# A hybrid decoder block on one core: x and mem loaded as columns, row scales put on the results, GpSimd taken out of two places

## The chip, the cores and the metric

The kernel runs on one core of a Trainium2 chip. A core has a matrix engine (TensorE, PE in the profile, with its weight loads as PEld), a vector engine (VectorE, DVE), an activation engine (ScalarE, ACT), a general engine (GpSimd, POOL) and SyncE (SP), which here issues every transfer between DRAM and on-chip memory. On-chip memory is SBUF (128 partitions) and PSUM (eight banks, where TensorE puts its sums). The metric is the device time of one execution in microseconds (us); the median of a kernel's runs is compared.

## The reference

All data is float32: x is 256 tokens of 1024 features, mem is 256 tokens of 1024.

```python
def rms_norm(x, g):
    y = xf * lax.rsqrt(jnp.mean(xf * xf, axis=-1, keepdims=True) + EPS)
    return (y * g)
h = x
hn = rms_norm(h, norm_mix)
(gq, gk, gv, gr, glr, nq, kc, vc, ks_, vs_, kw, vw, ng) = _split_cols(hn @ w_in)
o_gla = gla_mixer(gq, gk, gv, gr, glr, ...)      # 4 heads, chunked linear attention with decay
o_nsa = nsa_mixer(nq, kc, vc, ks_, vs_, kw, vw, ng, ...)  # 8 heads: compressed, selected, window
h = h + concat([o_gla, o_nsa]) @ w_out
h = h + cross_attn(rms_norm(h, norm_xattn), rms_norm(mem, norm_mem), ...)
h = h + peer_ffn(rms_norm(h, norm_ffn), ...)     # 8 heads pick 16 of 16384 experts per token
return rms_norm(h, norm_final)
```

The norm divides a row (a token) by its root mean square and multiplies a column (a feature) by g. A projection of the normed rows is therefore r(token) times (x * g) @ w: the row scale r can be applied after the projection as well as before it.

## The kernel before

**Numbers.** Every large product is done in three TensorE passes: each float32 factor is split in a high part (a rounded copy, made on ScalarE, line 137) and a low part (source minus high part, line 138, on VectorE or, where `eng` is P, on GpSimd); lines 152 to 154 multiply high by high, and the two mixed pairs. `weights` loads a 512 KB block of weights into one of four `raw` buffers and splits it into `whi` and `wlo`. `proj_t` multiplies one such block (8 pieces of 128 features) with the activations `xh`, `xl`, which lie as columns (feature on the partition, 256 tokens beside each other); its 24 products fill one of the two `pj` banks. `proj_n` does the same with tokens on the partition of the result.

**Stages, in the order of the program.**

1. x is loaded as rows (four DMAs), squared on ScalarE with the sums kept (line 170), `rstd_of` makes the row scale r by logarithm, exponential and one Newton step (lines 159 to 165); `norm_t` multiplies x by r and g (line 193, VectorE), turns it by TensorE transposes (line 197) and splits it into `xh`, `xl`.
2. `w_tok` (4 blocks of 296 KB, low parts on GpSimd) gives `tok`; `w_t` blocks 0 to 3 give qT and kT of the linear attention (scaled copies from PSUM on ScalarE). The gate goes from `tok` by transposes (line 297) and two products (line 304) to the decay.
3. Two rounds (d = 0 and 1) of linear attention: seven levels each, three or four VectorE operations per level (lines 366, 368, 373) between TensorE products (line 372). TensorE fills the time with `proj_t` blocks that are due later.
4. mem is loaded, normed and turned in the same way (lines 384 to 394) into `mh`, `ml`; compressed keys (lines 405 to 459), then queries nq and keys sk, copied out of PSUM by ScalarE.
5. Sparse attention, gates and output norm, cross-attention's keys and values, the output product, the norm between, cross-attention; `residual` adds each product to h and does the next norm. There `norm_t` of both halves is on the path: TensorE has nothing else that it may start.
6. PEER: eight `peer_wq` blocks (low parts on GpSimd), the search for the best keys on VectorE (`best`), then 128 `down_t` blocks, 256 weight maps and 128 `up` blocks. `gates_exp` needs another ScalarE table than the Gelu between whose uses it stands.
7. The last norm (lines 917 to 941): VectorE adds h, ScalarE squares, GpSimd multiplies by g (line 932), VectorE or ScalarE scales, four DMAs store.

**What sets the order.** The order on each engine is fixed when the program is built: the framework's scheduler lists the instructions by their dependences and its own estimate of times. `tc.issue_after(i)` adds that an instruction on i's engine stands behind i. SP issues all loads in one fixed order; a load into a `raw` buffer stands and waits until the buffer's last reader is done, and all that is behind it waits as well. `t8` tiles share two 8 KB buffers in turn, so mem's load waits for the second round of linear attention to let go of one.

## Time and profile before

| | us |
|---|---|
| median of 3 runs | 1105.44 (1105.41 to 1106.59) |
| profiled execution | 1104.22 |
| its span, first to last instruction | 1102.3 |
| TensorE busy | 1070.7 (97%) |
| VectorE busy | 775.8 (70%) |
| ScalarE busy | 583.8 (53%) |
| GpSimd busy | 113.9 (10%) |

A busy engine is one that has at least one instruction in it; TensorE's instructions overlap, so that the distance between starts tells its pace. A row of the timeline gives start, duration, engine, line, operation, the tile written and the tiles read, how many were merged, and in brackets how long the engine had been idle and what ended that. The granted clock is given as a share of full speed: 1.00 is 2.4 GHz, 0.50 is 1.2 GHz.

### The profile page before, as it was taken

The numbers are of one execution on the slowest core, as the hardware profiler recorded it, in microseconds if no ns is written. First come the engines' busy times: TensorE is split into PE (matmuls) and PEld (weight loads), VectorE is DVE, ScalarE is ACT, GpSimd is POOL, SyncE is SP. The second block draws the span as 40 slices with busy tenths as digits, with TensorE's granted clock in tenths as the row PEclk, the third lists the DMA queues.
The fourth block names the chain that finished last, engine by engine and source line by source line (L and its number), as shares of the span: only waits on it lengthen the run. The fifth ranks groups of instructions, "written<-read, shape, count | busy, mean of one in ns | idle before, by whom it ended". The sixth has DMA issues, their size and how long they took to land.

```text
span 1102.3 us, 20423 instructions
## 1 busy us (share of the span) xinstructions
PE 1070.7 (97%) x8174; PEld 963.6 (87%) x8174; DVE 775.8 (70%) x1454; ACT 583.8 (53%) x878; POOL 113.9 (10%) x71
## 2 busy tenths in 40 slices
PE   6999999999899999999999999999999999999996
PEld 5877789899699999999988888899999998888885
DVE  5764578576689698988666666566776766666665
ACT  5444445465455575666544444455655556444443
POOL 3303300000368700000000000000000000000001
PEclk9999999999899999999999999999999999999999
DMA  7623224663545654444565656655554545666663
GB/s 256 243 79 133 77 97 153 191 197 107 192 149 166 203 177 148 159 154 135 168 194 192 191 191 193 197 184 155 162 164 154 170 156 177 195 194 195 193 191 135
DMA packets 53564, 186.45 MB, mean 169 GB/s; under 512 B 6820, under 2 KB 8253, under 8 KB 53086
## 3 DMA queue, kind: packets, MB, share of 16 engines
q1 hardware_dynamic: 53470, 185.16, 53.1%
q8 instruction: 64, 1.05, 0.4%
q14 instruction: 30, 0.25, 0.1%
HBM read 182.76 MB, written 2.11 MB: 168 GB/s over the span
## 4 chain that ended last, share of the span: by engine, by line
PE 92%; DVE 4%; ACT 1%; DMA 1%; issue 1%; SPq 0%; POOL 0%; ACTq 0%; DVEq 0%; POOLq 0%
PE pj L152 15%; PE pj L153 15%; PE pj L154 15%; PE y L154 10%; PE y L153 10%; PE y L152 10%; PE pn L861 4%; PE po L152 1%; PE po L154 1%; PE po L153 1%; PE po L518 1%; PE pn L493 1%; PE pn L428 1%; PE pn L508 1%; DVE B L366 1%
## 5 line engine op out<-in xcount | busy, mean ns | idle before, releaser
L137 ACT ACTIVATE whi<-raw 128x1024 fp32r<-128x1024 f32 (+1 forms) x328 | 345.2, 1053 | 335.5 <-PE pj L153 163.4
L138 DVE TENSOR_TENSOR wlo<-raw,whi 128x1024 fp32r<-128x1024 f32 x288 | 352.2, 1223 | 186.7 <-ACT whi L137 185.6
L152 PE MATMUL pj<-xh,whi 128*128 128x256 f32 x1280 | 366.6, 287 | 1.4 <-ACT big L878 0.7
L154 PE MATMUL pj<-xh,wlo 128*128 128x256 f32 x1280 | 360.1, 281 | 0.2 <-DVE wlo L138 0.2
L153 PE MATMUL pj<-xl,whi 128*128 128x256 f32 x1280 | 360.3, 281 | 0.0
L154 PEld LDWEIGHTS pj<-xh,wlo 128*128 128x128 f32 x1280 | 244.6, 191 | 2.2 <-issue 1.4
L152 PEld LDWEIGHTS pj<-xh,whi 128*128 128x128 f32 x1280 | 241.5, 189 | 4.5 <-ACT big L878 1.2
L153 PEld LDWEIGHTS pj<-xl,whi 128*128 128x128 f32 x1280 | 241.5, 189 | 1.6 <-issue 1.0
L154 PE MATMUL y<-whi,Gl 128*128 128x512 f32 x512 | 199.4, 390 | 0.0
L153 PE MATMUL y<-wlo,Gh 128*128 128x512 f32 x512 | 199.4, 390 | 0.0
L152 PE MATMUL y<-whi,Gh 128*128 128x512 f32 x512 | 199.4, 389 | 0.0
L138 POOL TENSOR_TENSOR wlo<-raw,whi 128x1024 fp32r<-128x1024 f32 (+1 forms) x40 | 94.3, 2361 | 242.2 <-ACT whi L137 230.5
L154 PEld LDWEIGHTS y<-whi,Gl 128*128 128x128 f32 x512 | 96.2, 188 | 19.9
L153 PEld LDWEIGHTS y<-wlo,Gh 128*128 128x128 f32 x512 | 96.2, 188 | 19.8
L152 PEld LDWEIGHTS y<-whi,Gh 128*128 128x128 f32 x512 | 96.2, 188 | 19.8
L137 ACT ACTIVATE Gh<-big 128x512 fp32r<-128x512 f32 x64 | 40.5, 632 | 87.5 <-PE y L153 85.9
L138 DVE TENSOR_TENSOR Gl<-big,Gh 128x512 fp32r<-128x512 f32 x64 | 44.3, 693 | 51.7 <-ACT Gh L137 51.7
L932 POOL TENSOR_TENSOR wlo<-raw 128x512 f32<-128x512 f32 x4 | 5.0, 1278 | 710.8 <-DVE raw L930 710.8
L862 ACT ACTIVATE big<-pn 128x512 f32<-128x512 f32 x64 | 71.1, 1121 | 2.2 <-PE pn L861 2.2
L854 DVE TENSOR_TENSOR J<-OJ,gp 128x1536 bf16<-128x1536 bf16 x64 | 60.8, 951 | 0.0
L861 PE MATMUL pn<-J,OI 128*128 128x64 bf16 x1536 | 57.4, 194 | 0.3 <-DVE J L854 0.2
L861 PEld LDWEIGHTS <-OI 128*128 128x128 bf16 x1536 | 49.9, 98 | 3.5 <-DVE J L854 0.9
(622 smaller groups left out, 1122.2 us busy)
## 6 DMA issues: line engine op xcount, KB each, us to landing
raw<-down_t SPq DMA_DIRECT2D x128, 512.0 KB, 3.5
raw<-up SPq DMA_DIRECT2D x128, 512.0 KB, 4.2
raw<-w_t SPq DMA_DIRECT2D x16, 512.0 KB, 4.4
raw<-xa_wk SPq DMA_DIRECT2D x8, 512.0 KB, 3.5
raw<-xa_wv SPq DMA_DIRECT2D x8, 512.0 KB, 3.5
raw<-w_out SPq DMA_DIRECT2D x8, 512.0 KB, 4.3
raw<-xa_wq SPq DMA_DIRECT2D x8, 512.0 KB, 4.0
raw<-xa_wo SPq DMA_DIRECT2D x8, 512.0 KB, 3.4
```

The lines of the kernel that those rows point to most:

```text
L137: S.activation(hi, src, AF.Copy)
L138: last["lo"] = (eng or V).tensor_sub(lo, src, hi.bitcast(FT))
L152: TE.matmul(o, lh, rh, start=start, stop=False)
L153: TE.matmul(o, lh, rl, start=False, stop=False)
L154: last["mm"] = TE.matmul(o, ll, rh, start=False, stop=stop)
L366: V.tensor_mul(B[rows, :, l, r].rearrange("p t (b w) -> p t b w", w=hw), ev[rows, :, :, 1], qv[rows, :, :, 1])
L428: TE.matmul(p, R[:, l], w1[:, l], start=l == 0, stop=l == 15)
L493: TE.matmul(pA[:, :16 + ns], nq[r, m, ts_], sk[0][r, :16 + ns], start=True, stop=True)
L508: TE.transpose(pT[:, i * 128:(i + 1) * 128], pe[:, b, k * 128:(k + 1) * 128], ident)
L854: V.tensor_tensor(J.rearrange("p k g j t -> p (k g) j t"), OJ.rearrange("p g j t -> p (g j t)")[:, None].to_broadcast([128, 3, 512]), part ...
L861: TE.matmul(p[:, i], OI[:, g, :, q], J[:, k, g, :, q], start=k == 0, stop=k == 2)
L862: S.activation(W[:, :, ts_].rearrange("p j t -> p t j"), p, AF.Copy)
```

## The change

x comes in as columns (`x_t`) besides as rows, and so does mem (`mem_t`). `xh` and `xl` are made from the columns times g alone, in four pieces, each followed by its `w_tok` block, whose low part now is VectorE's. The rows of x are loaded behind that, only for the row scale r. `scales` leaves r in two forms: as a column per token (`rx`), and, by a product of a diagonal with a matrix of ones, as a row on all partitions (`rw`). Results with tokens on the partition are scaled while ScalarE copies them (`tok`, `gv`); results of `proj_t` are multiplied by `rw` on VectorE, which copies them out of PSUM in ScalarE's place (qT, kT, kc, nq, sk, gr: 16 of them). mem's columns are multiplied by g and r on VectorE and split, with no transposes.

In PEER's first stage the `peer_wq` blocks 1 and 2 are tied behind the last split of the norm's columns on ScalarE (before: behind the exponentials of the two row scales), and block 1's low part is VectorE's. `gates_exp` stands ten blocks later. In the last pair of `up` blocks the products are ordered by output piece. In the last norm the product with g is VectorE's.

```diff
+    g_t = mx.tile([128, 2, 8], FT, name="g_t")
+    nc.sync.dma_start(g_t, a["g_t"])
+    xt = t8([128, 8, T], "xt")
+    o = [pj()[:, :NTOK] for _ in range(2)]
+    for q in range(4):
+        nc.sync.dma_start(xt[:, 2 * q:2 * q + 2], a["x_t"][:, 2 * q:2 * q + 2])
+        for k in (2 * q, 2 * q + 1):
+            g = g_t[:, 0, k:k + 1]
+            S.activation(xh[:, k], xt[:, k], AF.Copy, scale=g)
+            V.scalar_tensor_tensor(xl[:, k], xt[:, k], g, xh[:, k].bitcast(FT), op0=OP.mult, op1=OP.subtract)
+        proj_n(a["w_tok"], xh, xl, NTOK, o, q, V)
+    x0 = t8([128, 2, D], "x0")
...
+    def scales(src, name, wide):
+        ssq = sums()
+        rows = mx.tile([128, 2], FT, name=name + "r")
+        p = pa()[:, :T]
+        for t in range(2):
+            for f in range(2):
+                square(src, src, t, f, ssq)
+            r = rstd_of(ssq[:, t, 1:2], ssq[:, t, 0:1])
+            V.tensor_copy(rows[:, t:t + 1], r)
+            diag = s2([128, 128], "diag")
+            V.tensor_scalar(diag, ident, r, 128.0, op0=OP.mult, op1=OP.mult)
+            TE.matmul(p[:, t * 128:(t + 1) * 128], onesd, diag, start=True, stop=True)
+        V.tensor_copy(wide, p)
+        return rows
...
-        S.activation(tok[:, t], o[t], AF.Copy)
+        S.activation(tok[:, t], o[t], AF.Copy, scale=rx[:, t:t + 1])
...
-        S.activation(qT[:, i], p, AF.Copy, scale=0.125)
+        V.scalar_tensor_tensor(qT[:, i], p, 0.125, rw, op0=OP.mult, op1=OP.mult)
...
-        S.activation(kT[:, i], p, AF.Copy)
+        V.tensor_mul(kT[:, i], p, rw)
...
-        norm_t(mt, r, sc, gam, mh, ml, [pa], t)
+    mw = s2([128, M], "mw")
+    scales(mt, "m", mw)
+    mc = t8([128, 8, M], "mc")
+    nc.sync.dma_start(mc, a["mem_t"])
+    for k in range(8):
+        V.scalar_tensor_tensor(mc[:, k], mc[:, k], g_t[:, 1, k:k + 1], mw, op0=OP.mult, op1=OP.mult)
+        if k % 2:
+            c = slice(k - 1, k + 1)
+            split(mc[:, c], mh[:, c], ml[:, c])
...
-            with tc.issue_after(after[hd - 1]) if hd in (1, 2) else nullcontext():
-                p = proj_t(a["peer_wq"][hd], xh, xl, P)
+            with tc.issue_after(after) if hd in (1, 2) else nullcontext():
+                p = proj_t(a["peer_wq"][hd], xh, xl, V if hd == 1 else P)
...
-            if hf == 0 and jj == LO_AT + 1:
+            if hf == 0 and jj == KEY_AT - 2:
                 gates_exp(gelu.ins)
...
+            if hf and jj == HALF - 2:
+                order = [(i, t, f) for t in range(2) for f in range(2) for i in range(2)]
...
-            P.tensor_mul(hg[t][:, w], hb[t][:, w], gfin[:, w])
+            V.tensor_mul(hg[t][:, w], hb[t][:, w], gfin[:, w])
...
-            if t and f:
+            if t and not f:
                 S.activation(hg[t][:, w], hg[t][:, w], AF.Copy, scale=r[t])
```

kc, nq, sk and gr change as kT does, gv as `tok` does; `after` is the last ScalarE split of the norm.

How the order moves, at three places. First SP's queue, the loads at the start; before:

```order
L133 DMA x_83<-x 128x512 x4
L134 DMA ident<-ident 128x128
L177 DMA raw<-gammas 128x1024
L268 DMA gw_165<-gla_gate_w 16x256
L269 DMA gw_165<-gla_gate_b 1x256
L143 DMA raw<-w_tok 128x592 x3
L281 DMA cst<-cst 128x586
L143 DMA raw<-w_tok 128x592
L283 DMA lev<-lev 128x1152
L143 DMA raw<-w_t 128x1024 x4
```

and now:

```order
L251 DMA g_t<-g_t 128x16
L260 DMA xt<-x_t 128x512
L137 DMA raw<-w_tok 128x592
L260 DMA xt<-x_t 128x512
L137 DMA raw<-w_tok 128x592
...
L269 DMA x_188<-x 128x512 x4
L270 DMA ident<-ident 128x128
...
L297 DMA cst<-cst 128x586
L299 DMA lev<-lev 128x1152
L137 DMA raw<-w_t 128x1024 x4
```

The broadcast g (`gammas`, 512 KB) is gone from the queue; x's rows stand between the last `w_tok` block and everything that `w_t` needs.

Second TensorE, from the last `w_tok` products to the first `w_t` block; before:

```order
L152 MATMUL pj<-whi,xh 128x296
L153 MATMUL pj<-wlo,xh 128x296
L154 MATMUL pj<-whi,xl 128x296
L152 MATMUL pj<-xh,whi 128x256
L153 MATMUL pj<-xl,whi 128x256
L297 MATMUL pa<-ident,tok 16x128
L154 MATMUL pj<-xh,wlo 128x256
```

and now:

```order
L146 MATMUL pj<-whi,xh 128x296
L147 MATMUL pj<-wlo,xh 128x296
L148 MATMUL pj<-whi,xl 128x296
L287 MATMUL pa<-diag,onesd 128x128
L313 MATMUL pa<-ident,tok 16x128
L287 MATMUL pa<-diag,onesd 128x128
L313 MATMUL pa<-ident,tok 16x128
L320 MATMUL pa<-gw_194,glr 128x256 x2
L146 MATMUL pj<-xh,whi 128x256
L147 MATMUL pj<-xl,whi 128x256
```

Both transposes of `tok` and the two gate products (line 304 before, 320 now) stand ahead of the first `w_t` block; before, one transpose and the gate products stood behind four blocks, at 33.6 us.

Third ScalarE in the norm before PEER (squares of h, the two row scales `r`, the splits `xh`); before:

```order
L170 ACTIVATE sc,ssq<-h 128x512 x2
L160 ACTIVATE r_2971<-ssq,r_2969 128x1
L162 ACTIVATE r_2971<-r_2971 128x1
L137 ACTIVATE whi<-raw 128x1024
L170 ACTIVATE sc,ssq<-h 128x512 x2
L160 ACTIVATE r_2982<-ssq,r_2980 128x1
L162 ACTIVATE r_2982<-r_2982 128x1
L137 ACTIVATE whi<-raw 128x1024
L137 ACTIVATE xh<-pa 128x2x128
L137 ACTIVATE xh<-pn 128x2x128
```

and now:

```order
L164 ACTIVATE sc,ssq<-h 128x512 x2
L154 ACTIVATE r_2954<-ssq,r_2952 128x1
L156 ACTIVATE r_2954<-r_2954 128x1
L164 ACTIVATE sc,ssq<-h 128x512 x2
L154 ACTIVATE r_2965<-ssq,r_2963 128x1
L156 ACTIVATE r_2965<-r_2965 128x1
L131 ACTIVATE xh<-pa 128x2x128
...
L131 ACTIVATE xh<-pn 128x2x128
L131 ACTIVATE whi<-raw 128x1024 x3
```

The two weight copies `whi` that stood inside the norm, each of which starts a GpSimd subtraction, are behind the last split of the columns.

## Rows read from the trace of the kernel before

**Rows 1.** Busy times by stretch: length, then PE, PEld, DVE, ACT, POOL; PEclk, DMA share, GB/s

```profile
0.00:22.70 22.70, 11.89 (x68) 10.97 (x68) 11.79 (x29) 12.42 (x29) 8.53 (x10) 1.00 0.77 253
22.70:95.10 72.40, 67.65 (x492) 59.13 (x492) 50.65 (x128) 32.19 (x68) 15.56 (x21) 1.00 0.50 169
290.90:304.10 13.20, 8.08 (x42) 6.69 (x42) 10.23 (x19) 5.63 (x16) 6.87 (x4) 0.74 0.70 247
1093.40:1102.30 8.90, 0.05 (x1) 0.00 (x0) 4.94 (x14) 2.66 (x7) 2.54 (x3) 0.76 0.32 118
```

**Rows 2.** The chain of waits at the start: start, us, what

```profile
10.83 3.36 POOL wlo L138 x2
14.19 6.01 DMA raw<-w_t
...
21.40 1.24 DVE wlo L138
22.68 0.39 PE pj L154
```

**Rows 3.** Busy times by stretch: the loads at the start

```profile
2.00:11.30 9.30, 1.18 (x6) 1.18 (x7) 3.62 (x13) 4.51 (x15) 0.47 (x1) 1.00 0.96 302
...
2.00:20.20 18.20, 9.72 (x54) 9.32 (x55) 9.93 (x23) 8.77 (x25) 8.12 (x5) 1.00 0.81 262
22.00:35.00 13.00, 12.78 (x107) 12.27 (x107) 6.62 (x10) 6.74 (x11) 0.43 (x2) 1.00 0.93 339
```

**Rows 4.** The timeline: x's last square to its row scale, and a copy of `tok`

```profile
6.43 0.63 ACT L170 ACTIVATE sc<-x 128x512 f32<-128x512 f32 x1 [0.22 <-DMA x<-x]
8.19 0.16 DVE L165 TENSOR_TENSOR r<-r,r 128x1 f32<-128x1 f32 x1
22.64 0.41 ACT L279 ACTIVATE tok<-pj 128x296 f32<-128x296 f32 x1
```

**Rows 5.** The timeline of TensorE in the first `peer_wq` block

```profile
300.77 0.42 PE L152 MATMUL pj<-xh,whi 128*128 128x256 f32 x1
300.98 0.42 PE L153 MATMUL pj<-xl,whi 128*128 128x256 f32 x1
...
303.45 0.28 PE L153 MATMUL pj<-xl,whi 128*128 128x256 f32 x1
303.57 0.28 PE L154 MATMUL pj<-xh,wlo 128*128 128x256 f32 x1
```

**Rows 6.** The chain of waits between 33 and 81 us

```profile
34.32 1.06 PE pa L304 x4
35.37 1.08 PE pa L340 x8
...
79.74 0.44 PE pa L197 x4
```

**Rows 7.** Groups by line, 286 to 304 us: count, busy us, mean ns

```profile
L193 DVE SCALAR_TENSOR_TENSOR sc<-h,r,raw 128x512 f32<-128x512 f32 x4 | 6.3, 1580 | 0.0
```

**Rows 8.** The timeline of the norm before PEER

```profile
291.37 2.34 POOL L138 TENSOR_TENSOR wlo<-raw,whi 128x1024 fp32r<-128x1024 f32 x1 [2.22 <-ACT whi L137]
291.60 2.66 DVE L193 SCALAR_TENSOR_TENSOR sc<-h,r,raw 128x512 f32<-128x512 f32 x1
294.24 0.73 DVE L193 SCALAR_TENSOR_TENSOR sc<-h,r,raw 128x512 f32<-128x512 f32 x1
301.69 0.43 DVE L138 TENSOR_TENSOR xl<-pn,xh 128x256 fp32r<-128x256 f32 x1
```

**Rows 9.** The timeline: TensorE behind the first Gelu after the exponential

```profile
394.43 0.39 PE L152 MATMUL pj<-xh,whi 128*128 128x256 f32 x1 [0.73 <-ACT big L878]
```

**Rows 10.** The timeline of the end

```profile
1092.24 1.22 DVE L161 SCALAR_TENSOR_TENSOR r<-ssq,r 128x1 f32<-128x1 f32 x1 [0.48 <-ACT whi L931]
1093.06 0.39 PE L154 MATMUL y<-whi,Gl 128*128 128x512 f32 x1
1098.06 0.72 ACT L938 ACTIVATE wlo<-wlo,r 128x512 f32<-128x512 f32 x1 [1.88 <-DVE r L165]
```

More of the change, by code (lines that the diff above doesn't have):

```diff
@@ L128, in s2 @@
         return fp.tile(shape, dt, name=name, tag="s2", bufs=6)
-    x0 = t8([128, 2, D], "x0")
-    for t in range(2):
-        for f in range(2):
-            nc.sync.dma_start(x0[:, t, f * 512:(f + 1) * 512], xv[:, t, f * 512:(f + 1) * 512])
-    nc.sync.dma_start(ident, a["ident"])
     def split(src, hi, lo, eng=None):
-        S.activation(hi, src, AF.Copy)
+        last["hi"] = S.activation(hi, src, AF.Copy)
         last["lo"] = (eng or V).tensor_sub(lo, src, hi.bitcast(FT))
@@ L246, in residual @@
             norm_t(h, r[t], sc, gam, xh, xl, ps, t, () if t else (add.ins,), scale)
-        return exps
-    ssq = sums()
-    sc = t8([128, 2, D], "sc")
-    for t in range(2):
-        for f in range(2):
-            square(x0, sc, t, f, ssq)
-        r = rstd_of(ssq[:, t, 1:2], ssq[:, t, 0:1])
-        if t == 0:
-            gam = gamma(0)
-        norm_t(x0, r, sc, gam, xh, xl, [pa, po], t)
-    show("xh", xh.bitcast(FT))
+        return last["hi"].ins
     mh = fp.tile([128, 8, M], FR, name="sh", tag="sh")
@@ L269, in body @@
     nc.sync.dma_start(gw2[16:], a["gla_gate_b"])
-    onesd = mx.tile([128, 128], FT, name="onesd")
-    P.memset(onesd, 1.0 / 128)
-    o = [pj()[:, :NTOK] for _ in range(2)]
-    for q in range(4):
-        proj_n(a["w_tok"], xh, xl, NTOK, o, q, P)
+    def scales(src, name, wide):
+        ssq = sums()
+        rows = mx.tile([128, 2], FT, name=name + "r")
+        p = pa()[:, :T]
+        for t in range(2):
+            for f in range(2):
+                square(src, src, t, f, ssq)
[6 more added lines that the diff above has]
+        return rows
+    rw = mx.tile([128, T], FT, name="rw")
+    rx = scales(x0, "x", rw)
     tok = mx.tile([128, 2, NTOK], FT, name="tok")
     for t in range(2):
-        S.activation(tok[:, t], o[t], AF.Copy)
+        S.activation(tok[:, t], o[t], AF.Copy, scale=rx[:, t:t + 1])
     cst = mx.tile([128, C_N], FT, name="cst")
@@ L385, in body @@
     nc.sync.dma_start(mt, a["mem"].rearrange("(t p) d -> p t d", p=128))
-    ssq = sums()
-    sc = t8([128, 2, D], "sc")
-    for t in range(2):
-        for f in range(2):
-            square(mt, sc, t, f, ssq)
-        r = rstd_of(ssq[:, t, 1:2], ssq[:, t, 0:1])
-        if t == 0:
-            gam = gamma(2)
-        norm_t(mt, r, sc, gam, mh, ml, [pa], t)
+    mw = s2([128, M], "mw")
[7 more added lines that the diff above has]
+            split(mc[:, c], mh[:, c], ml[:, c])
     bias = fp.tile([128, 8, 256], FT, name="bias", tag="h8")
@@ L414, in body @@
         kc = mx.tile([128, 2, T], FT, name="kc")
-        S.activation(kc[:, 0], p, AF.Copy)
+        V.tensor_mul(kc[:, 0], p, rw)
         for g in range(2):
@@ L554, in body @@
     for t in range(2):
-        S.activation(gv[:, t], o[t], AF.Copy)
+        S.activation(gv[:, t], o[t], AF.Copy, scale=rx[:, t:t + 1])
     gr = mx.tile([128, 4, T], FT, name="gr")
@@ L558, in body @@
         p = proj_t(a["w_t"][4 + i], xh, xl, P)
-        eg = mx.tile([128, T], FT, name="eg", bufs=2)
-        S.activation(eg, p, AF.Exp, scale=-1.0)
+        eg = s2([128, T], "eg")
+        V.tensor_mul(gr[:, i], p, rw)
+        S.activation(eg, gr[:, i], AF.Exp, scale=-1.0)
         V.tensor_scalar(eg, eg, 1e30, 1.0, op0=OP.min, op1=OP.add)
         V.reciprocal(eg, eg)
-        V.tensor_mul(gr[:, i], p, eg)
+        V.tensor_mul(gr[:, i], gr[:, i], eg)
     oh = fp.tile([128, 8, T], FR, name="oh", tag="oh")
@@ L904, in body @@
             split(g, *G)
-            end = hf and jj == HALF - 2
-            for i, t in ((0, 0), (1, 0), (0, 1), (1, 1)) if end else ((0, 0), (0, 1), (1, 0), (1, 1)):
+            order = [(i, t, f) for i in range(2) for t in range(2) for f in range(2)]
+            if hf and jj == HALF - 2:
+                order = [(i, t, f) for t in range(2) for f in range(2) for i in range(2)]
+            for i, t, f in order:
                 j = hf * HALF + jj + i
                 s = slice(t * 128, (t + 1) * 128)
-                for f in range(2):
-                    n = slice(f * 512, (f + 1) * 512)
-                    mm3(y[t][f], G[0][:, i, s], G[1][:, i, s], w[i][0][:, 0, n], w[i][1][:, 0, n],
-                        j == 0, j == NJ - 1)
+                n = slice(f * 512, (f + 1) * 512)
+                mm3(y[t][f], G[0][:, i, s], G[1][:, i, s], w[i][0][:, 0, n], w[i][1][:, 0, n], j == 0, j == NJ - 1)
         if hf == 0:
@@ L957, in by_n, with cols @@
         return A(w.reshape(4, 2, 128, f, n).transpose(3, 0, 2, 1, 4)).reshape(f, 4, 128, 2 * n)
+    def cols(v):
+        return A(v.reshape(v.shape[0], 8, 128).transpose(2, 1, 0))
     w = A(w_in)[0]
@@ L966, in arrange @@
         "x": A(x)[0], "mem": A(mem)[0], "rel_bias": A(rel_bias),
+        "x_t": cols(A(x)[0]), "mem_t": cols(A(mem)[0]),
+        "g_t": A(np.stack([A(norm_mix).reshape(8, 128), A(norm_mem).reshape(8, 128)]).transpose(2, 0, 1)),
         "ident": eye, "cst": cst, "u": u, "lev": lev,
```

8 lines of the change are left out of this document (6 added, 2 removed).

## The prediction

> **What bounds the kernel now.** I read the busy times by stretch first. TensorE is the bound nearly everywhere, so what counts is where it stands still: 22.70 − 11.89 = 10.8 us in the first stretch, 72.40 − 67.65 = 4.75 between 22.7 and 95.1 us, 13.20 − 8.08 = 5.1 around the norm before PEER, and 8.9 behind its last product [rows 1]. These 29.5 us are most of the 31.6 that TensorE is idle in the whole span (1102.3 less 1070.7 of the table); an edit helps where it shortens one of them or takes work off TensorE between them. Next the chain of waits at the start: two GpSimd subtractions (3.36 us) hold buffers, so that the first `w_t` block is asked for at 14.19 and lands at 20.20; its two splits follow, and TensorE runs without a break from 22.68 [rows 2]. Then the timelines of the norm and of the end, where small VectorE operations last several times their usual length while GpSimd works [rows 7, 8, 10].
>
> **The change part by part.**
>
> **Start.** The first product with a `w_t` low part was due at 20.20 plus 2.48 (two splits and their gaps) [rows 2]. Now 8 + 1024 + 1184 + 1024 + 64 + 17 + 293 + 576 KB stand ahead of that block's 512 KB in SP's queue (columns and scales, x's columns, `w_tok`, x's rows, identity, gate weights, constants, `lev`): 4702 KB, 4.82 MB. GpSimd no longer holds the buffers, so the transfers need not pause. At the 302 GB/s of the unbroken stretch they take 15.9 us from 2.0 on: landing 17.9, first low product 20.4, which is 2.3 earlier. The slowest nearby row, 262 with the pause in it, gives 22.9 (0.2 later), the fastest, 339, gives 18.7 (4.0 earlier) [rows 3]; I take 302, because the same kinds of transfers make it up. Two things must not be later than that. x's rows are through after 3.32 MB, at 13.0. From the start of the last square to r took 8.35 − 6.43 = 1.9, a copy of `tok` 0.41 [rows 4], the two gate products 1.06 [rows 6]; with 0.4 each for a transpose and a copy out of PSUM (estimates from the 0.43 of a 256-column VectorE operation [rows 8]) TensorE is through these at 17.2, before the block's high part at 19. And `lev` must be converted on VectorE before the first low part: it lands one block, 1.7 us, earlier, which is enough for an operation of about 1.5.
>
> TensorE, however, runs dry between the last `w_tok` product (that block lands after 2.27 MB, at 9.5) and 19. Around the norm before PEER it idled as long with a few transposes in between, the stretch's granted clock is 0.74 [rows 1], and afterwards products were 0.21 apart and not 0.12 [rows 5], so the array was at 1.2 and not 2.4 GHz there. Some 19 products at 0.09 more each cost 1.7; none gives 0, the block's remaining 22 give 2.0. Start: −2.3 + 1.7 = −0.6.
>
> The Trainium skill ("TensorE: Matmul & The Clock Gate", "HAM oscillation — how this bites in real kernels") says that matmuls which wait for data for long start the next block at the lower clock, every time. By that rule the total below stays as it is; with the clock kept up it would be 1.7 lower. The rows of the norm side with the rule.
>
> **Work that leaves TensorE between 22.7 and 95.1.** The gate products (1.06) move ahead of the first block, into idle time. mem's four groups of transposes go, 4 × 0.44 = 1.8; two products for its row scale come, 0.27 each by the four that take 1.08 [rows 6]. Net −2.3. Whether the 4.75 idle stay is the open point. 12 copies out of PSUM (4 of qT and kT, 2 kc, 4 nq, 2 sk) go from ScalarE, busy 32.19 of 72.40, to VectorE, busy 50.65 [rows 1]; at 0.43 [rows 8] that is 5.2. mem's eight column products and four splits take the place of four row products and eight splits. VectorE then has about 56 of 72. The kc copies stand at the end of each attention round, so that one of the two `pj` banks is held through it; on the other hand only 23 block products stand between the fourth block and the first round where 52 stood, so VectorE's long rounds start earlier. Behind the first copy of nq also waits mem's sum: mem's rows and columns are two transfers of 1 MB now, and TensorE reaches mem's first scale product soon after the second round, behind 16 products of the compression and 41 of nq. I put the idle time at 4.75 again; two of them less or three more are as far as I see.
>
> **The norm before PEER.** Four products with g took 6.3 us on VectorE [rows 7]; alone one takes 0.73, beside a GpSimd subtraction 2.66 [rows 8]. Now no subtraction lies there: its ScalarE part stands behind the last split. Four times 0.73 is 2.9, so VectorE saves 3.4, and ScalarE's second row scale is free of two copies of about 1 us. Walked through from the last add at 291.0: row products to 293.1, second scale 293.8, its products 295.0 and 296.5 with splits between, last low split near 298.9 and not 302.1 [rows 8]. TensorE's first block then ends at 301.1 to 302.0, with 12 to 22 of its products at the lower clock, against 304.0: −2.0 to −2.9, I take −2.5. If the clock held it would be −4. If block 1, whose high part now starts only at 298.4, came late (1.06 + 1.24 later, 300.7, is in time), it would eat 1.2 of the gain.
>
> **The exponential's tables.** They stand ten blocks later, where ScalarE has no key copies to make between. The 0.73 that TensorE waited [rows 9] may go: −0.7; another wait of that size the other way is the far end.
>
> **The end.** From the last product's end, 1093.45, to the last scaled piece, 1098.78, are 5.3 us [rows 10]. A one-column operation held up for 1.22 there is the stall that goes with GpSimd's products; those come to VectorE, 0.73 each [rows 8], and three of four stand before the last add. The piece that needs them is complete 0.7 earlier by the new order of products, which cancels one. −0.5, between −1.9 and +0.7.
>
> **Sum.** −0.6 − 2.3 − 2.5 − 0.7 − 0.5 = −6.6. The profiled execution took 1104.22, 1.9 around its span; 1097.6 there. The median of the runs is 1.2 above it: 1105.44 − 6.6 = 1098.8. The other `tok`, gv and gr changes fall into later stretches, where TensorE has next to no idle time; at worst each of four gr copies costs a 0.43 that is now covered by the next block.
>
> **The rivals.**
> - *TensorE keeps its clock, or the rounds have fewer gaps* (they start earlier): 1.7 more, 1097.1. For it: before, no fall shows in the first 95 us (1.00 [rows 1]). Against: the dry time is new.
> - *The loads are no faster than 262 GB/s*: the start gives +0.2 and, since TensorE then idles longer, the full clock cost: −6.6 + 2.9 = −3.7, 1101.7. For it: 2 KB pieces of x and `w_tok` alternate, and x is read twice. Against: the pause was the cause of 262.
> - *The long products with g were not GpSimd's doing* (the change doesn't do what it says): then only ScalarE's moved copies help, 1.0 and not 2.5 in the norm, and nothing at the end: 1100.8. Against: start and end of 2.66 fit the subtraction's [rows 8].
> - *Given back*: the gaps between 22.7 and 95.1 grow by 6, by mem's two transfers and the held banks: 1104.8, no change.
> - *Slower: VectorE's queue becomes the bound.* If TensorE waits at each of the 12 copies for a weight subtraction ahead of it, 1.24 [rows 2], that is 14.9: 1105.44 − 6.6 + 14.9 = 1113.7. It decides as soon as the copies come later than the 24 × 0.12 = 2.9 us that the second bank covers, at eight or more of the twelve. For it: the kc copies and the fuller VectorE. Against: 0.43 + 1.24 is under 2.9.
>
> **How the numbers follow.** A measurement of this kernel can tell about 0.2%, 2.2 us. Forecast 0.50 at 1098.8; clock or gaps 0.15; slow loads 0.14; GpSimd not the cause 0.05; given back 0.09; slower 0.07. Faster by over 0.2%: 0.84; within: 0.09; slower: 0.07. The range goes from 1094.3 (clock kept in both places and the far end of the tables and the end) to 1104.0, into the case of gaps that grow. The forecast's own range is 1096.5 to 1101.0.
>
> **What would show it.** The first `w_t` low product near 20.4; a granted clock of 0.50 for some us there; the sparse attention's first product, 95.1 before, near 92.2; all four products with g at about 0.73 and the first `peer_wq` block over near 301 less those 3 us; no 0.7 wait behind a Gelu; the last piece scaled some 4.8 us after the last product. The forecast is wrong if the idle time between the first `w_t` block and the sparse attention is over 10 us, or if a wait for DMA stands ahead of `w_t` past 22 us.

## The result, and the profile of the changed kernel

The changed kernel takes 1118.43 us (median of 4 runs, 1116.97 to 1118.85), the kernel before beside it 1105.43 (4 runs): a ratio of 1.0111, 95% interval 1.0092 to 1.013. It is slower by 13 us; the forecast was 1098.8, the range ended at 1104.0. The profiled execution's span is 1116.4 us against 1102.3.

The first view is again the busy time by stretch (length; PE, PEld, DVE, ACT, POOL busy with their counts; granted clock, DMA share, GB/s). It answers to [rows 1]:

```profile
0.00:22.70 22.70, 13.02 (x66) 11.25 (x67) 14.85 (x40) 14.93 (x31) 2.01 (x6) 0.97 0.84 288
22.70:95.10 72.40, 66.07 (x465) 56.83 (x465) 54.74 (x137) 27.02 (x48) 17.34 (x21) 0.97 0.51 174
95.10:118.00 22.90, 22.90 (x67) 15.59 (x66) 4.32 (x24) 5.91 (x19) 4.70 (x2) 0.53 0.11 42
175.00:185.00 10.00, 7.67 (x41) 5.70 (x40) 9.63 (x16) 2.74 (x5) 0.00 (x0) 0.83 0.01 2
305.10:318.20 13.10, 10.15 (x46) 8.29 (x45) 9.83 (x26) 7.80 (x20) 3.19 (x4) 0.74 0.55 201
```

The third row is the one to stop at. TensorE reads as busy all the time, 22.90 of 22.90 us, and yet the stretch is slow: its granted clock is 0.53, the lower of the two levels (1.2 instead of 2.4 GHz) for nearly all of it. A busy share alone would call this stretch perfect. The kernel before ran the same heads at 1.00, with 103 products in 21 us where the changed kernel starts 67 in 22.9:

```profile
95.00:116.00 21.00, 21.00 (x103) 14.91 (x103) 5.38 (x38) 10.40 (x35) 7.09 (x3) 1.00 0.23 76
```

Where the 14.1 us of span come from is read by setting the same product of TensorE in both timelines side by side (start of each, us):

| TensorE's product | before | after | shift |
|---|---|---|---|
| first with a `w_t` low part | 22.68 | 21.42 | -1.3 |
| first of the sparse attention | 95.02 | 96.50 | +1.5 |
| mem's keys, first block | 161.78 | 172.17 | +10.4 |
| mem's keys, third block | 178.02 | 194.95 | +16.9 |
| last of the second residual | 290.57 | 307.17 | +16.6 |
| last of the first `peer_wq` block | 303.91 | 318.74 | +14.8 |
| last blocks before the gates | 390.59 | 407.26 | +16.7 |
| block behind the gates' exponential | 394.43 | 410.32 | +15.9 |
| last product | 1093.06 | 1108.38 | +15.3 |
| end of the span | 1102.30 | 1116.45 | +14.1 |

The late edits together gain what they were to gain (-1.8, -0.8, -1.2; -3.8 in all against -3.7). Two places lose: 9 us in the sparse attention (+1.5 to +10.4) and 6.5 in mem's keys (+10.4 to +16.9). A third, +1.9 through the PEER blocks up to the gates, is a curiosity (at the end).

**Ahead of the sparse attention.** TensorE's timeline (start, us, engine, line, operation, tiles; in brackets the idle time before it and what ended it):

```profile
91.25 0.38 PE L465 MATMUL pn<-hid,w 128*128 128x32 f32 x2 [1.83 <-DVE hid L461]
...
94.74 0.66 PE L472 MATMUL pn<-w,hr 128*128 128x64 f32 x2 [1.76 <-issue]
...
96.50 0.85 PE L509 MATMUL pn<-sk,nq 64*128 64x144 f32 x2
```

Two waits of 1.8 us where the kernel before had one (1.79), and the second ends 1.8 us before the loop begins. Both wait for the gates of the compression, a chain of 30-column VectorE operations. The timelines of VectorE and GpSimd say why the chain is late; VectorE's, where L456 and L458 stand twice, once alone and once beside GpSimd:

```profile
87.51 2.37 DVE L456 TENSOR_TENSOR yy<-yy,xx 128x30 f32<-128x30 f32 x1
...
90.18 0.18 DVE L458 TENSOR_SCALAR yy<-yy 128x30 f32<-128x30 f32 x1
90.27 0.18 DVE L456 TENSOR_TENSOR yy<-yy,xx 128x30 f32<-128x30 f32 x1
...
91.76 1.81 DVE L458 TENSOR_SCALAR yy<-yy 128x30 f32<-128x30 f32 x1
```

```profile
86.77 3.06 POOL L132 TENSOR_TENSOR wlo<-raw,whi 128x1024 fp32r<-128x1024 f32 x1 [9.20 <-ACT whi L131]
91.17 2.37 POOL L132 TENSOR_TENSOR wlo<-raw,whi 128x1024 fp32r<-128x1024 f32 x1 [1.33 <-DVE hid L461]
```

An operation that takes 0.18 us at 90.27 takes 2.37 at 87.51, and ends at 89.88, 0.05 behind the end of GpSimd's subtraction (86.77 + 3.06 = 89.83); the other, 0.18 and 1.81, ends at 93.57, GpSimd at 93.54. These are the low parts of the first two `w_gv` blocks, which the change did not touch: it only moved the compression's chain under them. The same picture as [rows 8] of the norm, which the change did cure.

What that costs is in the clock (stretches, same columns as above):

```profile
88.00:92.00 4.00, 2.17 (x19) 2.00 (x18) 3.40 (x10) 1.29 (x3) 2.67 (x2) 1.00 0.24 58
92.00:96.00 4.00, 2.24 (x15) 2.07 (x14) 3.07 (x6) 0.00 (x0) 1.54 (x1) 0.62 0.86 315
96.00:100.00 4.00, 4.00 (x12) 2.66 (x12) 1.14 (x7) 1.46 (x4) 2.36 (x1) 0.50 0.05 22
100.00:116.00 16.00, 16.00 (x46) 10.70 (x45) 2.61 (x17) 4.09 (x16) 0.34 (x1) 0.50 0.10 34
116.00:120.00 4.00, 4.00 (x19) 2.94 (x18) 0.59 (x5) 1.59 (x7) 2.03 (x1) 0.90 0.23 65
```

Half busy for 8 us, then 0.50 until about 117 us, though the profile shows no wait behind 94.74: some 23 us at half speed.

**At mem's first keys.** VectorE's timeline around the fourth gr block (its row scaling is L577, the reciprocal of its gate L580), then TensorE behind it:

```profile
170.26 1.74 DVE L580 RECIPROCAL eg<-eg 128x256 f32<-128x256 f32 x1
...
173.40 1.75 DVE L580 RECIPROCAL eg<-eg 128x256 f32<-128x256 f32 x1
...
175.53 1.75 DVE L580 RECIPROCAL eg<-eg 128x256 f32<-128x256 f32 x1
177.19 0.37 DVE L577 TENSOR_TENSOR gr<-pj,rw 128x256 f32<-128x256 f32 x1
...
179.20 1.75 DVE L580 RECIPROCAL eg<-eg 128x256 f32<-128x256 f32 x1
```

```profile
177.62 0.38 PE L146 MATMUL pj<-sh,whi 128*128 128x256 f32 x1 [2.33 <-DVE gr L577]
```

The four chains of the output gate fall together behind the attention; a bank of TensorE's is read by an operation that stands behind three of them.

### The profile page after: what moved, and what is told of

The parts are those of the page before. It is cut to its first block, busy times and chain, and to the rows that moved or that the text cites. A ratio compares the mean times of both kernels' runs of the same rounds, so it can differ in the third digit from the quotient of the medians.

```text
span 1116.4 us, 20395 instructions
## 1 busy us (share of the span) xinstructions
PE 1085.3 (97%) x8150; PEld 971.7 (87%) x8150; DVE 783.2 (70%) x1485; ACT 582.1 (52%) x862; POOL 101.7 (9%) x62
## 4 chain that ended last, share of the span: by engine, by line
PE 89%; DVE 7%; ACT 2%; issue 1%; DMA 0%; SPq 0%; DVEq 0%; ACTq 0%
PE pj L146 15%; PE pj L147 14%; PE pj L148 14%; PE y L148 10%; PE y L147 10%; PE y L146 10%; PE pn L878 4%; PE po L148 1%; PE po L147 1%; PE po L146 1%; PE po L534 1%; PE pn L509 1%; PE pn L524 1%; PE pn L444 1%; DVE wlo L132 1%
## 5 line engine op out<-in xcount | busy, mean ns | idle before, releaser
L132 DVE TENSOR_TENSOR wlo<-raw,whi 128x1024 fp32r<-128x1024 f32 (+1 forms) x293 | 356.8, 1219 | 180.6 <-ACT whi L131 178.6
L148 PEld LDWEIGHTS y<-whi,Gl 128*128 128x128 f32 x512 | 96.1, 188 | 19.9
L147 PEld LDWEIGHTS y<-wlo,Gh 128*128 128x128 f32 x512 | 96.1, 188 | 19.9
L146 PEld LDWEIGHTS y<-whi,Gh 128*128 128x128 f32 x512 | 96.1, 188 | 19.8
L132 POOL TENSOR_TENSOR wlo<-raw,whi 128x1024 fp32r<-128x1024 f32 x35 | 85.8, 2455 | 223.0 <-ACT whi L131 221.3
L879 ACT ACTIVATE big<-pn 128x512 f32<-128x512 f32 x64 | 71.2, 1123 | 2.2 <-PE pn L878 2.2
L895 ACT ACTIVATE big<-pj 128x256 f32<-128x256 f32 x128 | 46.9, 367 | 0.0
```

The lines of the kernel that those rows point to most:

```text
L132: last["lo"] = (eng or V).tensor_sub(lo, src, hi.bitcast(FT))
L146: TE.matmul(o, lh, rh, start=start, stop=False)
L147: TE.matmul(o, lh, rl, start=False, stop=False)
L148: last["mm"] = TE.matmul(o, ll, rh, start=False, stop=stop)
L879: S.activation(W[:, :, ts_].rearrange("p j t -> p t j"), p, AF.Copy)
L895: gelu = S.activation(gl[:, jj], p, AF.Gelu_apprx_tanh)
```

## The experiments

The kernel before ran beside each: its medians are 1104.4 to 1104.7 us, against 1105.4 beside the changed kernel, so a difference between medians of different experiments can be off by about 1 us. In the diffs, V is VectorE, P is GpSimd, S is ScalarE, TE is TensorE.

**gv_vector, gr_first, gv_vector_gr_first: the first two repairs**

```diff
-        proj_n(a["w_gv"], xh, xl, 512, o, q, P)
+        proj_n(a["w_gv"], xh, xl, 512, o, q, V if q < 2 else P)
```

> The changed kernel with one edit: the first two of the four w_gv blocks have their low parts made by VectorE instead of GpSimd. Theory A (two GpSimd low parts, 86.8 to 89.8 and 91.2 to 93.5 us, hold up VectorE's 30-column operations of the compression gates, 0.18 us to 2.37 and 1.81 us; TensorE dries out for 1.83 and 1.76 us, and its clock then stays at 0.50 from 94 to 117 us): both operations take about 0.2 us, TensorE's two waits fall under 1 us together, the granted clock is 1.00 at 96 to 118 us, and the time is about 1106 us (1118.4 less 3 of waits and 9.5 of clock). Theory B (VectorE's own longer queue is what makes TensorE wait; GpSimd only happens to run): the 2.4 us of low parts come on top on VectorE, the waits stay at 3 us or more, the clock still falls, about 1118 to 1121 us.

Measured: 1119.63 us (1118.43 to 1122.62). No gain, and still not theory B. L456 fell to 0.19 us and the wait at 89 us is gone, but the third low part, still on GpSimd, now meets the last link of the chain. VectorE, then GpSimd, then TensorE:

```profile
92.49 2.41 DVE L470 COPY hr<-hid 128x128 f32<-128x128 f32 x1
```

```profile
92.47 2.34 POOL L132 TENSOR_TENSOR wlo<-raw,whi 128x1024 fp32r<-128x1024 f32 x1 [16.05 <-DVE sk L468]
```

```profile
95.00 0.41 PE L472 MATMUL pn<-w,hr 128*128 128x64 f32 x2 [1.70 <-issue]
```

One wait of 1.7 us at the start of the loop (four of its products stand ahead of the wait) was enough: the clock was 0.50 from about 97 us until 134, longer than in the changed kernel. So the number of waits isn't what sets the loss.

```diff
+        last["gr"] = V.tensor_mul(gr[:, i], p, rw)
+    for i in range(4):
         eg = s2([128, T], "eg")
-        V.tensor_mul(gr[:, i], p, rw)
         S.activation(eg, gr[:, i], AF.Exp, scale=-1.0)
-        V.tensor_scalar(eg, eg, 1e30, 1.0, op0=OP.min, op1=OP.add)
+        with tc.issue_after(last["gr"].ins):
+            V.tensor_scalar(eg, eg, 1e30, 1.0, op0=OP.min, op1=OP.add)
```

> The changed kernel with one edit: the four products of the output gate gr with the row scales (which free TensorE's banks) come first, and the four chains of exponential, clamp, reciprocal (1.75 us each) and product behind the last of them. Theory A (the fourth gr eviction, L577, ready about 166 us, stands in VectorE's queue behind three reciprocals until 177.2 us, so that TensorE waits 2.33 us for its bank and then runs at half clock until about 182 us): the wait and the fall of the clock at 175 to 185 us go, about 1113.5 us (5 less). Theory B (the bank isn't what TensorE waits for, the og chain behind it is): the reciprocals only move, the same wait comes a few us later, 1117 to 1119 us.

Measured: 1117.21 us (1116.25 to 1117.68), 1.2 less: theory B. The wait of 2.33 is gone and one of 2.6 stands at the next place, for the copy of og (L601), which now waits behind the same four reciprocals. Their order is not the trouble; that they come all at once is.

> Both edits together in the changed kernel. If the two losses are separate places, their gains add: about 1101 us (1118.4 less 12.5 less 5), under the kernel before. If the second is only pushed about by what the first does to the order, the sum falls short: 1105 or more.

Measured: 1118.55 us (10 runs, 1105.65 to 1123.35). No gain again, but its runs fall apart in two groups: three took 1105.7 to 1106.7 us at a mean granted clock of 0.990 or 0.991, seven 1118.3 to 1123.4 at 0.972 to 0.979. One program, one order of work, 12 us and more apart, with the clock.

**late_edits: the other half of the change, by itself,** as edits of the kernel before

```diff
-            with tc.issue_after(after[hd - 1]) if hd in (1, 2) else nullcontext():
-                p = proj_t(a["peer_wq"][hd], xh, xl, P)
+            with tc.issue_after(after) if hd in (1, 2) else nullcontext():
+                p = proj_t(a["peer_wq"][hd], xh, xl, V if hd == 1 else P)
...
-            if hf == 0 and jj == LO_AT + 1:
+            if hf == 0 and jj == KEY_AT - 2:
...
-            P.tensor_mul(hg[t][:, w], hb[t][:, w], gfin[:, w])
+            V.tensor_mul(hg[t][:, w], hb[t][:, w], gfin[:, w])
```

(and the order of the last two up tiles and ScalarE's piece, as in the change.)

> The kernel before with the changed kernel's edits behind the sparse attention alone: the second PEER block ordered behind the last split of the norm with its low parts on VectorE, the gates' exponential two steps later, the order of the last two up tiles, the last norm's products on VectorE and the piece that ScalarE scales. By the prediction's terms these are worth -2.5, -0.7 and -0.5, about 1101.7 us; by the shifts between the two traces (-0.8 at the norm before PEER, -0.8 at the gates, -1.2 at the end) about 1102.6; if they do nothing by themselves, 1105.4.

Measured: 1097.26 us (1097.03 to 1101.95), ratio 0.9935 (0.9917 to 0.9954). The late edits are good, by more than either estimate; the whole loss, and more, lies in the changes ahead of them.

**dense_ahead, dummy_fill: the clock apart from the waits**

```diff
+    ov_ = [pj() for _ in range(2)]
+    for q in range(2):
+        proj_n(a["w_gv"], xh, xl, 512, ov_, q, P)
...
-            TE.matmul(pA[:, :16 + ns], nq[r, m, ts_], sk[0][r, :16 + ns], start=True, stop=True)
+            with tc.issue_after(last["mm"].ins) if t + hd == 0 else nullcontext():
+                TE.matmul(pA[:, :16 + ns], nq[r, m, ts_], sk[0][r, :16 + ns], start=True, stop=True)
```

(and the loop keeps the last two `w_gv` blocks only.)

> The changed kernel with the same work in another order: the first two of the four w_gv blocks (24 products of 512 columns, 0.22 us each at full clock) stand in TensorE's queue between the two waits and the first product of the sparse attention, instead of among its heads. Both waits of 1.8 us stay. Theory A (a wait lets the clock fall, and what follows it decides how long it stays: back-to-back products bring it back in a few us, the sparse attention's small fp32 products, though TensorE reads busy, do not): the clock is back at 1.00 before 105 us instead of 117, and the time is 1109 to 1112 us. Theory B (the wait alone decides; the clock stays low for a fixed 23 us or more): no recovery before 117 us, 1117 to 1120 us.

Measured: 1107.67 us (10 runs, 1106.79 to 1109.2). Theory A. The waits are still there (1.8 and 1.1), the clock still falls, but it is back at 1.00 at 100 us, before the loop begins (103.81):

```profile
92.00:96.00 4.00, 2.90 (x16) 2.63 (x16) 2.84 (x6) 0.00 (x0) 2.12 (x1) 0.59 0.83 293
96.00:100.00 4.00, 4.00 (x14) 3.33 (x15) 1.11 (x2) 1.06 (x1) 1.83 (x1) 0.56 0.19 74
100.00:116.00 16.00, 16.00 (x77) 11.42 (x76) 3.57 (x25) 7.33 (x22) 6.04 (x4) 1.00 0.32 99
```

Compare the last row with the changed kernel's: 16.00 us busy in both, 77 products here and 46 there. The same work in another order saves 10.8 us (9.7 when each is taken against the kernel before beside it). The clock rose at 99.5 us, in the sixth of the 24 products of 512 columns, which stand in a row from 96.96 on. In the changed kernel such products stand one or two at a time among the loop's smaller ones until 115.37, then five in a row, and the clock rose there, at 116.8; in gv_vector it rose at 134.2, in a run of six (132.38 to 134.48). Such a run is no safeguard, though: in gv_vector the clock fell, at 96.7, in another run of six (95.99 to 97.72).

```diff
+    p = pn()
+    with tc.issue_after(last["mm"].ins):
+        for _ in range(14):
+            TE.matmul(p, xh[:, 0, :128], xh[:, 0:2].rearrange("p k t -> p (k t)"), start=True, stop=True)
+    p = p[:, :32]
     TE.matmul(p, w2[0], hid[0], start=True, stop=True)
```

(and the blocks of nq and sk come ahead of these lines.)

> The changed kernel with the end of the compression behind the sk projection in TensorE's queue, and 14 products of 512 columns that nothing reads (3.1 us) ahead of it, so that TensorE waits for the compression's gates at work instead of idle; VectorE and GpSimd do what they did. Theory A (the cost is the clock, not the wait): the clock stays at 1.00 from 92 to 120 us and the time is 1106 to 1108 us (1118.4 less 9.5 of clock less about 1). Theory B (the sparse attention itself, with more of its evictions on VectorE and with other neighbours, lets the clock fall): it falls in the loop all the same, 1117 to 1121 us.

Measured: 1115.21 us (10 runs, 1107.42 to 1119.23). A poor test: the products ended at 95.5, and the wait for hr (1.68 us, ending 97.28) stayed behind them, right ahead of the loop; the clock fell there. One run of the ten took 1107.42 at 0.993. It agrees with gv_vector, but tells the theories apart no further.

**chain_free, mem_rows: the cause of the waits**

```diff
-    V.tensor_copy(hr, hid[1][:, :, None, :].to_broadcast([128, 2, 4, 16]))
+    last["hr"] = V.tensor_copy(hr, hid[1][:, :, None, :].to_broadcast([128, 2, 4, 16]))
...
-        proj_n(a["w_gv"], xh, xl, 512, o, q, P)
+        with tc.issue_after(last["hr"].ins):
+            proj_n(a["w_gv"], xh, xl, 512, o, q, V if q < 2 else P)
```

> The changed kernel with the first two w_gv low parts on VectorE, and these behind the last operation of the compression's chain (hr) in VectorE's queue, so that neither GpSimd nor a long VectorE operation stands in the chain. Theory A (GpSimd's two low parts make the chain late): the 30-column operations take about 0.2 us, TensorE's waits before the sparse attention fall under 1 us, the clock stays at 1.00, about 1106 us. Theory B (the chain is late by VectorE's queue ahead of it, mem's scaling and the evictions, whatever GpSimd does): a wait of 1.5 us or more stays and the clock falls as before, 1116 to 1120 us.

Measured: 1103.31 us (10 runs, 1102.22 to 1104.94): 15 us less than the changed kernel and level with the kernel before (ratio 0.9994, 0.998 to 1.0009), theory A. The chain, in VectorE's timeline, and TensorE's first product of the loop:

```profile
87.32 0.18 DVE L456 TENSOR_TENSOR yy<-yy,xx 128x30 f32<-128x30 f32 x1
...
89.51 0.17 DVE L458 TENSOR_SCALAR yy<-yy 128x30 f32<-128x30 f32 x1
...
90.52 0.23 DVE L470 COPY hr<-hid 128x128 f32<-128x128 f32 x1
```

```profile
91.82 0.51 PE L509 MATMUL pn<-sk,nq 64*128 64x144 f32 x2
```

No operation of the chain is stretched, TensorE has no wait there, the loop begins at 91.8 and the clock is 1.00 from 26 to 160 us. What is left is the second loss, unchanged: 2.33 us behind gr and a clock of 0.83 from 160 to 170.

> The changed kernel with mem normalised by rows and turned round by TensorE as in the kernel before (mem_t, its row of scales and mc are gone; x keeps its columns). If mem's scaling on VectorE at 79 to 85 us is what makes the compression late: the two waits shrink to the one of 1.8 us of the kernel before, the clock stays, about 1107 us. If the row scales of x on the evictions do it (kc, nq, sk on VectorE): 1117 to 1120 us.

Measured: 1104.29 us (10 runs, 1103.07 to 1106.51). This too cures the first loss, but not for the reason I gave. TensorE has no wait between 84 and 100 us; GpSimd's first `w_gv` low part starts at 89.45 there, when the chain is over. Handling mem by rows shifts the meeting of the two; that is what its trace shows.

**eg_own: the cause of the second loss**

An edit on top of chain_free:

```diff
-        eg = s2([128, T], "eg")
+        eg = mx.tile([128, T], FT, name="eg", bufs=1)
```

> chain_free with one more edit: the output gate's tile eg has a buffer of its own again (one) instead of its turn in the ring of six that it shares with the sparse attention's tiles. Theory A (in that ring eg gets a buffer only when the last heads' tiles are done, so all four chains of exponential, clamp, reciprocal and product, 2.2 us each on VectorE, fall together behind the loop at 170 to 181 us, whatever their order): the chains spread over the loop as in the kernel before, the wait of 2.3 us and the half clock behind it go, about 1099 us (1103.3 less 2.3, less 1.1 for the waits on kl, less 1.7 of clock). Theory B (VectorE has no room for them in the loop): 1102 to 1104 us.

Measured: 1098.8 us (6 runs, 1098.23 to 1099.19), ratio 0.995 (0.9936 to 0.9964): theory A, to 0.2 us. The four reciprocals stand apart again, as in the kernel before (133.49, 139.53, 149.29 and 161.61 there):

```profile
130.31 1.75 DVE L581 RECIPROCAL eg<-eg 128x256 f32<-128x256 f32 x1
137.70 1.75 DVE L581 RECIPROCAL eg<-eg 128x256 f32<-128x256 f32 x1
146.61 1.75 DVE L581 RECIPROCAL eg<-eg 128x256 f32<-128x256 f32 x1
154.78 1.74 DVE L581 RECIPROCAL eg<-eg 128x256 f32<-128x256 f32 x1
```

The change had moved eg from two buffers of its own into the ring `s2`, whose tiles go round in program order: eg's turn comes behind the last head's. One buffer of its own is enough to part the four.

**norm_fill, both_fill: what the clock costs at the other two places**

```diff
+    def fill(p, a_, n, *ins):
+        with behind(*ins):
+            for _ in range(n):
+                TE.matmul(p, a_[:, 0, :128], a_[:, 0:2].rearrange("p k t -> p (k t)"), start=True, stop=True)
...
             p = ps[f % len(ps)]()
+            if idle and f == 0:
+                fill(p, idle[0], idle[1][t], last["tr"] if t else last["mm"].ins)
```

> eg_own with products that nothing reads in TensorE's two waits in the norm before PEER (7 of 512 columns ahead of the first four transposes, 4 ahead of the third four; about 0.22 us each). Theory A (the waits of 1.5 and 0.9 us let the clock fall to 0.50 for about 7 us, worth 3.5 us): the clock stays at 1.00 there, about 3 us less than eg_own. Theory B (the waits are what costs, and they stay): same as eg_own, or 0.3 us more.

Measured: 1097.32 us (6 runs, 1096.44 to 1099.14), 1.5 less than eg_own. Theory A, half the size. eg_own's row for the norm, then norm_fill's:

```profile
290.00:300.00 10.00, 8.16 (x50) 7.09 (x51) 7.03 (x17) 6.42 (x15) 3.59 (x3) 0.83 0.60 215
```

```profile
290.00:300.00 10.00, 9.15 (x62) 7.35 (x61) 7.37 (x18) 7.19 (x16) 3.59 (x3) 1.00 0.65 233
```

The clock that came back is 0.17 of 10 us, 1.7: the row gives the gain, and my 3.5 came from a longer fall in another trace.

> norm_fill with 6 more such products between the second and the third product of the first w_t block at the start (TensorE waits 1.22 us there for the low part, then runs at half clock for about 4 us, worth 2 us). Theory A: the clock stays at 1.00 through 26 us, 1.5 to 2 us less than norm_fill. Theory B (the clock falls there because the waits before it, 0.36, 0.38 and 0.64 us, already thinned TensorE's work, or for the small products between them): no change, within 0.5 us of norm_fill.

Measured: 1096.26 us (6 runs, 1095.5 to 1097.44), 1.1 less; ratio to the kernel before 0.9925 (0.9911 to 0.9939), the best version. Its clock is 1.00 from 18 to 26 us where eg_own shows 0.89 and 0.68.

**before_gpsimd: the same fault made in the kernel before**

```diff
-        p = proj_t(a["w_t"][14 + i], xh, xl)
+        p = proj_t(a["w_t"][14 + i], xh, xl, P if i == 0 else None)
```

> The kernel before with one edit: the low part of the first sk block (w_t block 14), at about 86 us, by GpSimd instead of VectorE. Theory A (GpSimd's operations in the compression's chain are the cause of the loss, in any kernel): VectorE's small operations beside it take about 2 us each, TensorE's wait before the sparse attention grows from 1.8 to 3.5 us or more, the clock falls to 0.50 in the loop, 1112 to 1118 us. Theory B (before has slack there: dense products follow the wait and the clock holds or comes back): 1106 to 1109 us, only the wait.

Measured: 1109.0 us (10 runs, 1105.97 to 1110.87), ratio 1.0039 (1.0025 to 1.0052). Theory B. The wait grew to 2.54 us, longer than either ahead of the loop in the changed kernel, and the clock held:

```profile
88.00:92.00 4.00, 1.74 (x16) 1.54 (x14) 3.26 (x5) 1.18 (x3) 2.36 (x1) 1.00 0.31 115
92.00:96.00 4.00, 3.73 (x32) 3.63 (x32) 0.82 (x2) 1.33 (x2) 1.56 (x1) 1.00 0.38 131
```

Between the wait's end and the loop (92.27 to 95.97) stand 29 products of the sk projection here, against 5 in the changed kernel (94.74 to 96.50). So the length of a wait does not set the loss either. The edit did less than it was meant to: the low part that it moves ran on GpSimd at 79.66, ahead of the compression's gates, where it held up a row product of mem's norm (L193, 2.09 us). What is held up in the gates (L442, 2.33 us) stands beside the first `w_gv` low part, as in the kernel before (1.87).

Nor does a block behind the wait always keep the clock up. In the trace of late_edits_fill (below), whose front is that of the kernel before, a wait of 1.88 was followed by a fall from 92.6 to 96.1 us, among the same products of the sk projection:

```profile
90.00:100.00 10.00, 8.41 (x42) 7.08 (x42) 2.61 (x10) 3.44 (x8) 5.26 (x3) 0.83 0.33 107
```

In dense_ahead, too, it fell behind the first wait, at 92.7, ahead of the second. When a wait lets the clock fall is therefore open; what these traces show is how long the fall lasts: over by 96.1 us with the projection behind it, until 116.8 us with the loop.

The longer wait and a new one of 0.91 at 82 us are 1.7 of the 4.6 us that the edit costs; the rest I did not trace.

**columns_only, late_edits_fill: the prediction's two sums**

columns_only is eg_own with the diff of late_edits taken back; late_edits_fill is late_edits with the products of norm_fill.

> eg_own with the changed kernel's late edits (PEER block order, gates, last up tiles, last norm) undone, so that only x and mem as columns and the row scales remain, with the two repairs. Theory A (the prediction's sums for the front and the late part hold once the two losses are gone: about -2.9 and -3.7): about 1101.5 us, under the kernel before by 2.5 to 3.5. Theory B (the late edits are worth the 7 us that late_edits showed by itself, and the columns nothing or less): 1104.5 to 1106 us.

Measured: 1102.13 us (12 runs, 1100.39 to 1104.57), ratio 0.9971 (0.9958 to 0.9985), 2.6 less than the kernel before (1104.72): theory A. And eg_own, which adds the late edits, is 3.3 under it.

> late_edits with the 11 products that nothing reads in the norm before PEER. Theory A (three of the four runs of late_edits, at 1097.2 us and a mean clock of 0.999, already kept the clock in that norm; the fourth, at 1101.95 and 0.993, lost it there and at 80 us): the products make the clock of that norm 1.00 in every run, the time is 1096.5 to 1097.5 us with no run above 1100. Theory B (the clock there had nothing to do with the fast runs, their gain lies in the front): 1095 us or less for the fast runs, as norm_fill gained 1.5 us on eg_own.

Measured: 1098.26 us (6 runs, 1096.98 to 1101.01). Neither theory in full. The norm's clock is 1.00 (290 to 310 us), but the profiled run lost it elsewhere (0.83 at 90 to 100 us, ahead of the sparse attention) and one run was above 1100. It is no faster than late_edits, so late_edits' 1097 runs had nothing left to win at the norm; by their mean clock of 0.998 or 0.999, against 0.990 to 0.995 in the kernel before, they lost it next to nowhere. They were not profiled, so where they kept it is inferred.

## Why the prediction was wrong, point by point

**The step that failed** is the one the prediction called the open point: "I put the idle time at 4.75 again". It came to 72.40 - 66.07 = 6.3 us. That is within the three more that were allowed for, and as idle time it would have cost 1.6. What was not thought of is what idle time does at that place. I priced a fall of the clock at the start, where a block of products follows and it costs 2 us, and not ahead of the sparse attention, where it cost about 9 (+1.5 to +10.4 in the table): dense_ahead got those back with two waits still there, chain_free by removing both. Its price was not fixed by the program: by time and mean clock, gv_vector_gr_first escaped it in three of ten runs, the changed kernel in none of four. The prediction's own test (wrong if the idle time is over 10 us) looked at the size of the wait and would not have seen it.

**Why the idle time moved** was in the rows already. [Rows 8] show a VectorE operation at 2.66 beside a GpSimd subtraction, and the kernel before had one such meeting in the compression, its wait of 1.79. I took GpSimd out of the norm and the end and did not ask which other VectorE chains the change would bring under the GpSimd operations that stay. The Trainium skill ("SBUF — State Buffer", "SBUF: two separate sides") says that VectorE and GpSimd share a pair of ports as an exclusive lock, held for a whole instruction, against operations with two SBUF inputs or in a two-port mode. The ends that coincide to 0.03 to 0.09 us agree with that, for a product of two SBUF tiles (L456), a one-input TENSOR_SCALAR (L458) and a copy (L470 in gv_vector); whether the last two ran in a two-port mode the traces don't show.

**Start, -0.6.** The clock fell as said (0.50 to 0.70 from 22 to 26 us in the traces with the new start and no products to fill it), and both_fill puts it at 1.1 us, not 1.7. The first low product came at 21.42, not 20.4. In the trace of late_edits, whose start is that of the kernel before, it comes at 21.14, against 22.68 [rows 2]: executions differ by as much as the term.

**Work that leaves TensorE, -2.3.** Right in total, and by luck. Without the stretched operations the sparse attention begins at 91.82; the forecast said 92.2. But in eg_own, from the first low product (21.14) to the sparse attention (91.58), TensorE is busy 67.60 of 70.44 us, in the kernel before 67.58 of 72.34. The busy time is the same, with a half clock in it that both_fill puts at 1.1, so the work that left is worth about 1.1 (an estimate from these rows) and not 2.3. The idle time, which the prediction left at 4.75, fell to 2.8: the wait of 1.79 is gone.

**The copies on VectorE.** The slower rival (1113.7) had the sign right and the mechanism wrong: of the twelve copies it spoke of, the changed kernel's list of TensorE's waits names none between 20 and 130 us. A wait of that kind did come, 2.33 us, at a thirteenth copy in a stretch that the prediction settled in a sentence ("at worst each of four gr copies costs a 0.43 that is now covered"). That sentence looked at the copy and not at the line above it in the diff, where eg changes its ring; it cost up to 6.5 in the trace, and 4.5 between chain_free and eg_own.

**Norm before PEER, -2.5.** Held, a little smaller: -1.8 in the table. All four products with g take 0.74 us; the group by line, which answers to [rows 7]:

```profile
L187 DVE SCALAR_TENSOR_TENSOR sc<-h,r,raw 128x512 f32<-128x512 f32 x4 | 2.9, 744 | 0.0
```

**Tables, -0.7.** The number came, -0.8, and no wait of TensorE's is left there [rows 9]; that the edit did it is not shown. In seven traces that have the same edit, late_edits (402.27) and chain_free among them, TensorE still waits 0.73 or 0.74 behind a Gelu, some 15 us ahead of the exponential's tables; in columns_only, which lacks the edit, it waits 0.19.

**End, -0.5.** It gave -1.2. The last scaled piece, which answers to [rows 10], ends at 1112.57, 3.8 behind the last product's end (1108.77), where 4.8 was forecast and 5.3 stood before:

```profile
1108.38 0.39 PE L148 MATMUL y<-whi,Gl 128*128 128x512 f32 x1
...
1111.85 0.72 ACT L955 ACTIVATE wlo<-wlo,r 128x512 f32<-128x512 f32 x1 [0.88 <-DVE r L159]
```

**The sum.** -2.9 in front and -3.7 behind were right as totals: columns_only measures -2.6, the late edits on top of it -3.3, the repaired whole 1098.8, which is the forecast. To the tenth that is luck: in front two terms were off in opposite ways, as said above, and eg_own is another kernel than the one forecast. The 13 us were lost to two things outside the sum. The late edits by themselves gave 7.2; the 3.5 beyond their sum goes with a higher mean clock, and why the front of the kernel before should keep its clock better with them is open.

## What to carry to other kernels

A wait of the bounding engine is priced by what stands behind it, not by its length alone: with a block of projections behind them, a wait of 2.5 us left the clock alone in one trace and one of 1.9 cost it until 96 us in another; one of 1.7 at the start of a loop of small products cost some 10 us more than itself. So after moving work look for the waits that end right before such a loop, and put a block of projections between, as dense_ahead does. When an operation is taken from an engine that blocks another, list every other operation that stays on it and what the change now brings beside it. And read a tile's pool in a diff as closely as its engine: a shared ring ties a tile's start to the last user ahead of it in program order, however early its inputs are ready.

## What the runs showed of the chip that was not expected

- TensorE at 100% busy and half clock for 23 us (37 in gv_vector) without a wait that the profile shows: 46 products in 16 us against 77 to 82 at full clock. The Trainium skill ("TensorE: Matmul & The Clock Gate", "HAM oscillation — how this bites in real kernels") tells of a kernel in which waits for data of about 3 to 5 us make each next block start at the lower clock. A wait of that length stands in the norm before PEER of the kernel before, 3.35 us, and agrees: the clock of that stretch is 0.74 [rows 1]. Shorter waits, of 1.7 to 1.9 us, were followed by a fall in the changed kernel, gv_vector and late_edits_fill, and one of 2.54 us in before_gpsimd was not.
- The same program can fall on either side: gv_vector_gr_first took 1106 or 1118 to 1123 us, and its mean granted clock was 0.99 or 0.97 to 0.98.
- At a granted clock of 1.00 the products of a `peer_wq` block were 113.3 ns apart from 340 to 400 us in the kernel before, and 117.8 in the changed kernel, with operands of the same shapes; behind the gates it was the other way for a while. That is the +1.9 of the table, of which 0.6 came back. What sets it was not tried.
